# Modulation vectors by multiply-and-sum along rows on the vector engine instead of matrix products: all of layer 1's and two thirds of layer 0's, the latter in the delta-rule part

## The chip, the cores and the metric

The kernel runs on one core of a Trainium2 chip. The core has a matrix engine (PE, with its weight loads shown apart as PEld), a vector engine (DVE), a scalar engine (ACT), a general engine (POOL) and a sync engine (SP) that here does nothing but start DMA transfers. Each engine works through its own list of instructions strictly in that list's order; an instruction whose inputs are late holds up everything behind it in the same list. The metric is the device time of one execution in microseconds (us), as a median over runs.

## The reference, cut to what matters

Two layers run over 512 latent tokens and 256 context tokens of 1024 channels. In each layer every normalisation and every residual is modulated by six vectors per token kind, which come from one condition vector for the latent tokens (`c`) and one for the context tokens (`c_ctx`):

```
def adaln_modulation(cond, w_mod, b_mod):
    m = jax.nn.silu(cond) @ w_mod + b_mod          # (1024) @ (1024, 6144) + (6144)
    return jnp.split(m[..., None, :], N_MOD, axis=-1)
...
    sh1, sc1, g1, sh2, sc2, g2 = adaln_modulation(c, w_mod[layer], b_mod[layer])
    csh1, csc1, cg1, csh2, csc2, cg2 = adaln_modulation(c_ctx, w_mod[layer], b_mod[layer])
    h = rmsnorm(x, norm1_g[layer]) * (1.0 + sc1) + sh1
    ...                                             # input projection, three mixers, merge
    x = x + g1 * mix
    x = x + g2 * sq_relu_mlp(rmsnorm(x, norm2_g[layer]) * (1.0 + sc2) + sh2, ...)
```

`sh1` and `sc1` are needed at the start of a layer, `g1`, `sh2`, `sc2`, `g2` only after the mixers. The last layer's context tokens need `csh1` and `csc1` alone. The three mixers of a layer are a state-space scan (S5), a windowed attention, and a gated delta rule, which inverts small triangular matrices and then takes 12 sequential steps over chunks of tokens.

## The kernel before

All weights come from DRAM in tiles of 128 x 1024 floats (512 KB). `load_w` (L221) brings one in by SP's queue (tile `ws`, three buffers, L217), rounds it on ACT (`wh`, L227) and forms the rest on DVE (`wl`, L228; in some parts on POOL); a product is then three PE passes into PSUM (`pg`, L178: `wh` with the high part of the activations, `wl` with the high part, `wh` with the low part). The tiles `wh` and `wl` have two buffers each.

The modulation vectors of a layer are 6144 numbers for two token kinds. `adaln` (L241) makes them in 12 blocks of 512 columns. A block is four transfers of 512 KB (`wa`, SP's queue), eight PE products that stream 512 columns each with the 32 columns of conditions (`conds`) as weights, in 32-column strips of PE (L251, 16 rows of the profile to a block since each 32-bit product counts twice), one ACT scaling (`ms`, L254), four PE transposes (L257), and two short DVE instructions (`md`, `modv`). `adaln` is a generator: each `drain` puts one more block into the program. Layer 0's blocks 2, 3, 0, 1 stand at the start. Layer 0's blocks 4 to 11 stand in the conv part of layer 0, one before the keys of the attention and one behind each projection with its convolution (`conv`). Layer 1's 12 blocks stand in layer 0's MLP, one at every second of the up products; the tables for layer 1's scan (`s5_tables`, many short DVE instructions) stand there too.

Layer 0 goes in this order, by the profile's time: start and input projection for the scan (to about 214 us); the conv part, in which DVE carries the S5 scan (L669 to L672, a chain of short instructions) and PE the projections (to about 395); the attention (to about 597); the delta-rule part (`dn_main`, to about 920); the merge of the three mixers (to about 1110); and the MLP (to about 1760), which has four groups of eight up products and eight down products. Layer 1 follows.

The delta-rule part has these steps. *Prep*: the keys are transposed, their square sums taken on DVE (`dsq`, L1022), masks multiplied (`dD`, `dLT`, `dQK`). SP then writes the triangular blocks to DRAM and reads them back in another layout (`dl`, `dN`). *Inversion*: 31 rounds of a product and a subtraction on DVE for both directions (`dtm` L1123, `dPi` L1125). SP writes the inverse out and reads it back (`dp`, `dq`, `dLT`, `dPT`), PE and DVE join the blocks (L1147, L1157, `dLT` L1164). *Core*: 12 sequential steps of small PE products with DVE, ACT and POOL between. *Out*: normalisation and transposes. Since this chain leaves PE free for long stretches, 28 large products that nothing there waits for (the gates, `gates` in `mixers`) are put between by `place`: its plan `G0` gives for each a mark (an instruction of the chain), behind which the scheduler may put it. Eight of them have the mark `p5`, the last product of the prep, so that they cover the inversion.

A scheduler decides the order on each engine from the order in the program, these marks and its own model of durations.

Of the kernel before, what the change touches and what calls it, by code (L numbers as in the profile page):

```python
# [8 lines left out]
F32 = mybir.dt.float32  # L9
F32R = mybir.dt.float32r  # L10
I32 = mybir.dt.int32
AF = mybir.ActivationFunctionType
OP = mybir.AluOpType
# [4 lines left out]
NL = 2  # L18
# [15 lines left out]
SM_G1, SM_G2, SM_GF, SM_BM, SM_CV, SM_DG, SM_SK, SM_AL, SM_DT, SM_D = 0, 16, 32, 40, 136, 256, 258, 274, 290, 306  # L34
# [6 lines left out]
def pack(inp):  # L41
    import numpy as np

    f = {k: np.asarray(v) for k, v in inp.items()}
    o = {}

    def feat(a):
# [6 lines left out]
    cond[:, 1] = f["c_ctx"]  # L54
    o["cond"] = feat(cond.T)
    o["wmod"] = np.ascontiguousarray(
        f["w_mod"].reshape(NL, 4, 2, 128, 12, 512).transpose(0, 4, 1, 3, 2, 5).reshape(NL, 12, 4, 128, 1024))

    cg = (128 * np.arange(4)[:, None, None] + 16 * np.arange(8) + np.arange(16)[:, None]).reshape(-1)
    idx = list(cg)  # L60
# [64 lines left out]
    t = np.arange(128)[:, None]  # L125
# [56 lines left out]
def setup(g):  # L182
    tc, nc, A = g.tc, g.nc, g.A
    es = g.es
    g.base = es.enter_context(tc.tile_pool(name="base", bufs=1))
    g.wp = es.enter_context(tc.tile_pool(name="wp", bufs=2))
    g.ps = es.enter_context(tc.tile_pool(name="ps", bufs=1, space=PSUM))
    g.dr = es.enter_context(tc.tile_pool(name="dr", bufs=1, space=DRAM))
    g.ca = g.base.tile([128, CA_N], F32, name="ca")
    nc.sync.dma_start(g.ca, A["ca"])  # L190
    g.sm = g.base.tile([128, SM_N], F32, name="sm")
    nc.sync.dma_start(g.sm, A["small"])
    g.ident = g.ca[:, CA_ID:CA_ID + 128]
    g.ones = g.base.tile([128, 32], F32, name="ones")
    nc.gpsimd.memset(g.ones, 1.0)
    g.cneg = g.base.tile([128, 1], F32, name="cneg")
    nc.gpsimd.memset(g.cneg, -0.5)
    g.cpos = g.base.tile([128, 1], F32, name="cpos")
    nc.gpsimd.memset(g.cpos, 0.5)
    g.hpi = g.base.tile([128, 1], F32, name="hpi")  # L200
    nc.gpsimd.memset(g.hpi, math.pi / 2)
    g.modv = g.base.tile([128, NL, 48, 2], F32, name="modv")
    g.g1 = g.base.tile([128, 8, 2], F32, name="g1a")
    g.g2 = g.base.tile([128, 8, 2], F32, name="g2a")

# [26 lines left out]
def cond_setup(g):  # L232
    nc = g.nc
    c = g.p5a[1].tile([128, 8, NCH], F32, name="cond", tag="uy", bufs=2)[:, :, :32]
    nc.sync.dma_start(c, g.A["cond"])
    g.cs = g.base.tile([128, 8, 32], F32, name="conds")
    nc.scalar.activation(g.cs, c, AF.Tanh, scale=0.5)
    nc.vector.scalar_tensor_tensor(g.cs, g.cs, 1.0, c, op0=OP.add, op1=OP.mult)


def adaln(g, l, nbs, pool, bufs=2):  # L241
    nc = g.nc
    for nb in nbs:
        ps = pm(g, "s")
        for kp in range(4):
            w = pool.tile([128, 1024], F32, name="wa", tag="wa", bufs=bufs)
            g.ad_last = nc.sync.dma_start(w, g.A["wmod"][l, nb, kp])
            for k2 in range(2):
                kt = kp * 2 + k2
                c = kt % 4  # L250
                nc.tensor.matmul(ps[32 * c:32 * c + 32, :], lhsT=g.cs[:, kt, :], rhs=w[:, k2 * 512:k2 * 512 + 512],  # L251
                                 start=kt < 4, stop=kt >= 4, tile_position=(0, 32 * c))
        ms = pool.tile([128, 512], F32, name="ms", tag="ms", bufs=1)
        nc.scalar.mul(ms, ps, 0.5)  # L254
        p2 = pm(g, "s")
        for j in range(4):
            nc.tensor.transpose(p2[:, j * 128:j * 128 + 128], ms[:, j * 128:j * 128 + 128], g.ident)  # L257
        md = pool.tile([128, 4, 2], F32, name="md", tag="md", bufs=1)
        nc.vector.tensor_reduce(md, raw(p2, 0, [[128, 4], [1, 2], [32, 4]]), axis=AX.X, op=OP.add)
        bm = g.sm[:, SM_BM + 48 * l + nb * 4:SM_BM + 48 * l + nb * 4 + 4]  # L260
        nc.vector.tensor_tensor(g.modv[:, l, nb * 4:nb * 4 + 4, :], md,
                                bm[:, :, None].to_broadcast([128, 4, 2]), op=OP.add)
        yield


def drain(it, n=1):
    for _ in range(n):
        next(it, None)
# [1032 lines left out]
def mixers(g, l, hp):  # L1301
    g.marks = {}
    nc, tc, A = g.nc, g.tc, g.A
    cx = l < NL - 1
# [77 lines left out]
    if cx:  # L1382
# [6 lines left out]
        pa = pa_.__enter__()  # L1389
        with tc.tile_pool(name=f"a1{l}", bufs=1, side="right", reuse_waits="tile") as a1:  # L1390
            att_setup(g, l, pa, pa, a1, cx)
            ad = adaln(g, 0, range(4, 12), a1, AD1)
            drain(ad)
            att_kv()
            for x, i in enumerate(list(range(4, 12)) + list(range(4))):
                conv(i, a1, CDV0[x])
                drain(ad)
                if x in HS:
                    with tc.issue_after(g.wl_last) if HI else nullcontext():
                        g.hst.pop(0)()  # L1400
            bat = dn_ba(g, l, a1)
# [9 lines left out]
        pa_.__exit__(None, None, None)  # L1411
        s5_close()
        g.wle = nc.vector

        def fill(wh):
            if wh == "out":
                place(g, gt, G0, H0, sum(GU0.values()))

        dn(bat, fill)
        fl_.__exit__(None, None, None)  # L1420
        hp[0].__exit__(None, None, None)
    else:
# [276 lines left out]
def mlp(g, l, out):  # L1699
# [4 lines left out]
    if cx:  # L1704
        tb = s5_tables(g, l + 1, lambda k, d: nc.vector, 1)
    with tc.tile_pool(name=f"ml{l}", bufs=1, reuse_waits="tile") as pool:
        ad = adaln(g, l + 1, range(12), pool)
        def up(js, grps):
            ws = [load_w(g, l, W_F1 + j) for j in js]
            rs = [pool.tile([128, nn], F32, name="rl", tag="rl", bufs=2) for _ in js]  # L1710
# [11 lines left out]
        for gi in range(4):  # L1722
            hid = []
            for j in range(8):
                if gi > 0 or j > 1:
                    up([8 * gi + j], groups(cx))
                elif j == 0:
                    up([0, 1], [[p] for p in passes(cx)])
                if cx:
                    drain(ad, j % 2)  # L1730
                    drain(tb)
            last = gi == 3 and not cx
            if last:
                g.mp_.__exit__(None, None, None)
                last_group(g, l, pool, hid, out)
                break
            sts = [Stats(g, pool, p.n, 2, ("rl", nn), "ms", p.key) for p in P_LC] if cx and gi == 3 else None
            ws = {}
            order = [(m, p) for m in range(8) for p in (P_LC if cx else P_LC[:1])]
            if sts:  # L1740
                order = order[:12] + [(m, p) for p in P_LC for m in (6, 7)]
            for m, p in order:
                if m not in ws:
                    ws[m] = load_w(g, l, W_F2 + 8 * gi + m)
                ff2(g, l, ws[m], m, p, hid)
                if sts:
                    sts[P_LC.index(p)].add(m, g.x[:, m, p.sl])
                    if m == 7:
                        st = sts[P_LC.index(p)]
                        g.pbs.append(st.bcast())  # L1750
                        if PF and p.key == "l":
                            st.pace(PF)
                        else:
                            g.plan = []
# [90 lines left out]
```

## Time and profile before

| | |
|---|---|
| median of three runs | 2936.27 us (2933.69, 2936.27, 2941.55) |
| the profiled execution | 2948.86 us, of which the span of the instructions is 2947.1 us |
| PE busy | 2703.7 us, 92% of the span |
| PEld busy | 2190.6 us, 74% |
| DVE busy | 1664.9 us, 56% |
| ACT busy | 908.2 us, 31% |
| POOL busy | 595.6 us, 20% |
| DMA transfers | 343.61 MB, mean 117 GB/s |

Busy time is the union of an engine's instructions; products on PE overlap, so that 100% busy is not PE at its peak. Durations in the text are from the one profiled execution, which was 12.6 us longer than the median.

### The profile page before, as it was taken

What the parts mean: (1) busy time and instruction counts of PE and PEld (TensorE: products, weight loads), DVE (VectorE), ACT (ScalarE), POOL (GpSimd) and SP (SyncE); (2) the same over time, 40 slices, a digit from 0 to 9 for tenths busy, and PEclk for the clock granted to TensorE, in tenths of its full rate; (3) what the DMA queues carried; (4) which work ended last, traced back from release to release, by engine and by line L of the source; (5) the groups of instructions that cost most, each with busy time, mean ns of one, the idle gap of its engine ahead of it and who ended that gap; (6) DMA issues with size and microseconds to landing.
All of it is one profiled execution on the core that took longest, in us unless ns stands there. A gap on an engine that the chain in (4) does not pass through costs nothing.

```text
span 2947.1 us, 46158 instructions
## 1 busy us (share of the span) xinstructions
PE 2703.7 (92%) x17844; PEld 2190.6 (74%) x17844; DVE 1664.9 (56%) x4335; ACT 908.2 (31%) x1643; POOL 595.6 (20%) x765
## 2 busy tenths in 40 slices
PE   4698799999999999999999999758996999999998
PEld 1585578878677788787778878646775768889997
DVE  7839984345336647747432334996457368444443
ACT  2243343233222323223121324332342233323322
POOL 4643331030213300000000011532253133100001
PEclk8799898799999999999999999878997999999999
DMA  6564422236116433535341234123433226232222
GB/s 225 154 229 159 141 72 87 69 117 172 54 39 200 132 120 115 164 120 152 118 135 66 67 113 157 65 71 116 139 100 79 95 69 213 88 99 95 94 94 72
DMA packets 206619, 343.61 MB, mean 117 GB/s; under 512 B 89280, under 2 KB 121152, under 8 KB 206400
## 3 DMA queue, kind: packets, MB, share of 16 engines
q1 hardware_dynamic: 171712, 297.56, 31.5%
q0 software_dynamic: 9600, 36.71, 3.8%
q10 hardware_dynamic: 25088, 6.40, 1.0%
q8 instruction: 140, 2.29, 0.3%
q14 instruction: 79, 0.65, 0.1%
HBM read 269.04 MB, written 68.16 MB: 114 GB/s over the span
## 4 chain that ended last, share of the span: by engine, by line
PE 66%; DVE 10%; issue 3%; POOL 1%; DMA 1%; ACT 1%; SPq 1%; POOLq 0%; DVEq 0%; ACTq 0%
PE pg L178 46%; PE pg L1577 4%; DVE rt L669 2%; PE ps L697 1%; DVE st L672 1%; PE ps L251 1%; PE pm L1200 1%; DVE rt L671 1%; PE pm L1231 1%; PE ps L849 1%; PE pm L1209 1%; PE ps L858 1%; PE pg L1627 1%; PE ps L1246 1%; PE ps L1219 1%
## 5 line engine op out<-in xcount | busy, mean ns | idle before, releaser
L228 DVE TENSOR_TENSOR wl<-ws,wh 128x1024 fp32r<-128x1024 f32 x234 | 291.9, 1249 | 339.0 <-ACT wh L227 303.7
L227 ACT CAST wh<-ws 128x1024 fp32r<-128x1024 f32 x272 | 284.9, 1049 | 609.6 <-PE pg L178 473.9
L178 PE MATMUL pg<-hhil,wh 128*128 128x512 f32 x720 | 296.2, 412 | 52.4 <-ACT cxp L884 35.2
L178 PE MATMUL pg<-hlol,wh 128*128 128x512 f32 x720 | 293.7, 408 | 0.7 <-DVE hlol L367 0.7
L178 PE MATMUL pg<-hhil,wl 128*128 128x512 f32 x720 | 292.3, 406 | 0.0
L178 PE MATMUL pg<-hlo,wh 128*128 128x512 f32 (+1 forms) x800 | 282.5, 353 | 6.2 <-DVE hlo L367 6.2
L178 PE MATMUL pg<-hh,wh 128*128 128x512 f32 (+1 forms) x832 | 284.9, 344 | 3.0 <-DVE x L1674 2.6
L178 PE MATMUL pg<-hhi,wh 128*128 128x512 f32 (+1 forms) x800 | 283.0, 354 | 4.9 <-ACT cxp L884 4.9
L178 PE MATMUL pg<-hh,wl 128*128 128x512 f32 (+1 forms) x832 | 284.2, 343 | 1.0 <-DVE wl L228 1.0
L178 PE MATMUL pg<-hl,wh 128*128 128x512 f32 (+1 forms) x832 | 283.7, 342 | 0.0
L178 PE MATMUL pg<-hhi,wl 128*128 128x512 f32 (+1 forms) x800 | 280.5, 351 | 0.0
L178 PEld LDWEIGHTS pg<-hhil,wh 128*128 128x128 f32 x720 | 139.4, 194 | 97.1 <-ACT cxp L884 36.7
L1674 DVE SCALAR_TENSOR_TENSOR x<-pg,modv,x 128x512 f32<-128x512 f32 (+1 forms) x104 | 64.9, 626 | 246.0 <-PE pg L178 245.7
L178 PEld LDWEIGHTS pg<-hlo,wh 128*128 128x128 f32 x800 | 155.9, 195 | 37.4 <-issue 13.8
L178 PEld LDWEIGHTS pg<-hh,wh 128*128 128x128 f32 x832 | 157.3, 189 | 30.1 <-issue 8.3
L178 PEld LDWEIGHTS pg<-hhi,wh 128*128 128x128 f32 x800 | 155.7, 195 | 31.6 <-issue 8.8
L178 PEld LDWEIGHTS pg<-hhi,wl 128*128 128x128 f32 x800 | 155.6, 195 | 29.4 <-issue 11.5
L178 PEld LDWEIGHTS pg<-hh,wl 128*128 128x128 f32 x832 | 157.4, 189 | 24.5 <-issue 4.1
L178 PEld LDWEIGHTS pg<-hl,wh 128*128 128x128 f32 x832 | 157.4, 189 | 23.3 <-issue 5.6
L178 PEld LDWEIGHTS pg<-hhil,wl 128*128 128x128 f32 x720 | 139.2, 193 | 35.9 <-issue 4.8
L178 PEld LDWEIGHTS pg<-hlol,wh 128*128 128x128 f32 x720 | 139.2, 193 | 35.3 <-issue 4.9
L178 PE MATMUL pg<-hhic,wh 128*128 128x256 f32 x400 | 114.2, 286 | 3.9 <-ACT cxp L884 3.0
(438 smaller groups left out, 6019.9 us busy)
## 6 DMA issues: line engine op xcount, KB each, us to landing
ws<-in_wt SPq DMA_DIRECT2D x272, 512.0 KB, 3.6
wa<-in_wmod SPq DMA_DIRECT2D x96, 512.0 KB, 4.4
gtd<-gr POOLq DMA_DIRECT2D x24, 384.0 KB, 2.9
tg<-gtd POOLq DMA_DIRECT2D x24, 384.0 KB, 3.4
tb<-tC SPq DMA_DIRECT2D x64, 128.0 KB, 2.3
cvd<-ctp SPq DMA_DIRECT2D x20, 384.0 KB, 2.6
gtd<-gr POOLq DMA_DIRECT2D x24, 256.0 KB, 2.5
tg<-gtd POOLq DMA_DIRECT2D x24, 256.0 KB, 3.0
```

The source lines that it names most:

```text
L178: g.nc.tensor.matmul(ps, lhsT=wt[:, a], rhs=x(k), start=i == 0, stop=i == n - 1)
L227: nc.scalar.copy(hi, s)
L228: g.wle.tensor_tensor(lo, s, hi.bitcast(F32), op=OP.subtract)
L251: nc.tensor.matmul(ps[32 * c:32 * c + 32, :], lhsT=g.cs[:, kt, :], rhs=w[:, k2 * 512:k2 * 512 + 512], start=kt < 4, stop=kt >= 4, tile_pos ...
L669: v.tensor_tensor(t1, view(k - 1), A12[:, 0], op=OP.mult)
L671: v.tensor_tensor(t1, t1, view(k), op=OP.add)
L672: v.tensor_tensor(view(k), t1, t2, op=OP.add)
L697: nc.tensor.matmul(o, lhsT=gm[pp, k * 128:k * 128 + 128], rhs=st[pp, k // 2, k % 2, pr, c0:], start=False, stop=k == 3)
L849: nc.tensor.transpose(p[:, x * 128:x * 128 + 128], Ps[kv][:, i * 128:i * 128 + 128], g.ident)
L858: mi = nc.tensor.matmul(po[64 * kv:64 * kv + 64, :128], lhsT=a.v[:, kt, 64 * kv:64 * kv + 64], rhs=PT[:, 2 * i + kv, :], start=i == 0, sto ...
L1577: nc.tensor.matmul(ps, lhsT=wt[:, a], rhs=x[:, k, sl], start=i == 0, stop=i == 11)
L1674: g.nc.vector.scalar_tensor_tensor(g.x[:, m, sl], acc, g.modv[:, l, 40 + m, p.r:p.r + 1], g.x[:, m, sl], op0=OP.mult, op1=OP.add)
```

## The change

Twenty of the 24 blocks are no longer made by PE. A second copy of the modulation matrix is kept transposed in DRAM (`wmodt`): a tile there is 128 output features on the partitions by the 1024 inputs along the row. The two condition vectors lie beside it, repeated on all partitions (`condr`, 1 MB). A new generator, `adaln_rows`, makes their silu once (two ACT and two DVE instructions of 128 x 1024) and then, for each tile, one transfer of 512 KB and one DVE instruction `tensor_tensor_reduce` of 128 x 1024 for each token kind, which multiplies the tile by the condition and sums along the row, onto the bias, straight into `modv`. In the profile such an instruction is followed by a short one that reads the accumulator out.

Layer 0's blocks 4 to 11 become 32 tiles with two instructions each (64 in all). They leave the conv part and go into the delta-rule part, two tiles with each of the first eight gates and one with each later one, in a pool with one buffer for `wa` and one for the product `wo`. Since they are drained inside `place`, they stand behind the same marks as the gates. Layer 1's blocks become 48 tiles, of which 16 have two instructions and 32 have one (64 in all), two buffers for `wa`, in layer 0's MLP: two tiles with each of the first 20 up products, one with the others. The four blocks at the start stay.

```
+def adaln_rows(g, l, tiles, nr, pool, bufs=2):
+    nc = g.nc
+    c = pool.tile([128, 2, 1024], F32, name="condr", tag="condr", bufs=1)
+    nc.sync.dma_start(c, g.A["condr"])
+    for r in range(2):
+        w = pool.tile([128, 1024], F32, name="wa", tag="wa", bufs=bufs)
+        nc.scalar.activation(w, c[:, r], AF.Tanh, scale=0.5)
+        nc.vector.scalar_tensor_tensor(c[:, r], w, 1.0, c[:, r], op0=OP.add, op1=OP.mult)
+    yield
+    for t in tiles:
+        w = pool.tile([128, 1024], F32, name="wa", tag="wa", bufs=bufs)
+        nc.sync.dma_start(w, g.A["wmodt"][48 * l + t - 16])
+        b = SM_BM + 48 * l + t
+        for r in range(nr(t) - 1, -1, -1):
+            o = pool.tile([128, 1024], F32, name="wo", tag="wo", bufs=1) if r else w
+            nc.vector.tensor_tensor_reduce(o, w, c[:, r], 0.5, g.sm[:, b:b + 1], op0=OP.mult, op1=OP.add,
+                                           accum_out=g.modv[:, l, t, r:r + 1])
+        yield
...
             att_setup(g, l, pa, pa, a1, cx)
-            ad = adaln(g, 0, range(4, 12), a1, AD1)
-            drain(ad)
             att_kv()
             for x, i in enumerate(list(range(4, 12)) + list(range(4))):
                 conv(i, a1, CDV0[x])
-                drain(ad)
...
         g.wle = nc.vector
+        ad_ = tc.tile_pool(name=f"ad{l}", bufs=1, side="right", reuse_waits="tile")
+        ad = adaln_rows(g, l, range(16, 48), lambda t: 2, ad_.__enter__(), 1)
+
+        def gates_ad():
+            for i, _ in enumerate(gt):
+                drain(ad, 2 if i < 8 else 1)
+                yield
 
         def fill(wh):
             if wh == "out":
-                place(g, gt, G0, H0, sum(GU0.values()))
+                place(g, gates_ad(), G0, H0, sum(GU0.values()))
+                drain(ad, 40)
...
-        ad = adaln(g, l + 1, range(12), pool)
+        if cx:
+            ad = adaln_rows(g, l + 1, range(48), lambda t: 2 if t < 16 else 1, pool)
...
-                    drain(ad, j % 2)
+                    drain(ad, 1 + (j + 8 * gi < 20))
```

What the scheduler makes of it is shown at three places. The first is DVE's list in the inversion of layer 0 (`dtm` and `dPi` are the rounds of the inversion in its two directions, `wl` belongs to a gate's weights). Before, some rounds in a row stand so:

```order
L1123 TENSOR_TENSOR dtm_5836<-dN_5780,dPi_5781 96x192
L1123 TENSOR_TENSOR dtm_5839<-dN_5789,dPi_5790 96x192
L1125 TENSOR_TENSOR dPi_5781<-dPi_5781,dtm_5836 96x24x8
L1125 TENSOR_TENSOR dPi_5790<-dPi_5790,dtm_5839 96x24x8
L1123 TENSOR_TENSOR dtm_5842<-dN_5780,dPi_5781 96x207
L1123 TENSOR_TENSOR dtm_5845<-dN_5789,dPi_5790 96x207
L228 TENSOR_TENSOR wl<-ws,wh 128x1024
L1125 TENSOR_TENSOR dPi_5781<-dPi_5781,dtm_5842 96x23x9
L1125 TENSOR_TENSOR dPi_5790<-dPi_5790,dtm_5845 96x23x9
```

Now:

```order
L1146 TENSOR_TENSOR dtm_5606<-dN_5568,dPi_5569 96x135
L284 ISA wo,modv<-wa,condr,sm 128x1024
L284 ISA modv 128x1
L1148 TENSOR_TENSOR dPi_5578<-dPi_5578,dtm_5597 96x29x3
L1148 TENSOR_TENSOR dPi_5569<-dPi_5569,dtm_5606 96x27x5
L284 ISA wa,modv<-wa,condr,sm 128x1024
L284 ISA modv 128x1
L1146 TENSOR_TENSOR dtm_5603<-dN_5577,dPi_5578 96x112
L1146 TENSOR_TENSOR dtm_5612<-dN_5568,dPi_5569 96x156
L1148 TENSOR_TENSOR dPi_5578<-dPi_5578,dtm_5603 96x28x4
L1148 TENSOR_TENSOR dPi_5569<-dPi_5569,dtm_5612 96x26x6
L231 TENSOR_TENSOR wl<-ws,wh 128x1024
```

Between the first and the last round of the inversion stand 18 of the new instructions (nine pairs) and seven `wl`; before there were four `wl`. Of the other 46, three stand ahead of the first square sum (`dsq`), 11 between it and the last `dQK`, six between that and the first round, seven between the last round and the last joining copy `dLT`, and 19 in the first steps of the core (counted in the whole list, by the new instruction's line).

The second place is SP's list of transfers, from the write of the triangular blocks (`dl`) to the write of the inverse (`dp`). Before:

```order
L1107 DMA dl<-dLT 32x24x32 x8
L1357 DMA dvf<-cvd_1081 128x768 x2
L217 DMA ws<-in_wt 128x1024
L1111 DMA dN_5780<-dl 96x1024
L1111 DMA dN_5789<-dl 96x1024
L1380 DMA dzg<-zgd_1082 128x768 x2
L217 DMA ws<-in_wt 128x1024 x5
L1128 DMA dp<-dPi_5781 96x1024
```

Now:

```order
L1130 DMA dl<-dLT 32x24x32 x8
L280 DMA wa<-in_wmodt 128x1024
L1380 DMA dvf<-cvd_1082 128x768 x2
L220 DMA ws<-in_wt 128x1024
L280 DMA wa<-in_wmodt 128x1024
L1134 DMA dN_5568<-dl 96x1024
L1134 DMA dN_5577<-dl 96x1024
L280 DMA wa<-in_wmodt 128x1024
L220 DMA ws<-in_wt 128x1024
L280 DMA wa<-in_wmodt 128x1024
L220 DMA ws<-in_wt 128x1024
L280 DMA wa<-in_wmodt 128x1024
```

The list goes on in that way, one `wa` to one `ws`, up to the write of the inverse, and behind the 14 transfers of the inverse ten more `wa` stand ahead of the next `ws`. With one buffer, each `wa` waits until both instructions on the tile before it are done.

The third place is DVE's list at the end of the scan in the conv part (`rt` and `st` are the scan, `aP` and `aM` the attention's scores and maxima, `gr` a gate). Before:

```order
L669 TENSOR_TENSOR rt_2144<-st,A_1337 128x64
L670 TENSOR_TENSOR rt_2145<-st,A_1337 128x64
L671 TENSOR_TENSOR rt_2144<-rt_2144,st 128x64
L751 TENSOR_TENSOR arf<-arf,ash 128x512
L672 TENSOR_TENSOR st<-rt_2144,rt_2145 128x2x32
L825 ISA aP,aM<-pm,cb,sm 128x384
```

Now:

```order
L1390 SCALAR_TENSOR_TENSOR gr<-gr,pg 128x256
L695 TENSOR_TENSOR st<-rt_2139,rt_2140 128x2x32
L862 TENSOR_SCALAR aP<-aP,aM 128x256 x2
L1391 TENSOR_SCALAR gr<-gr 128x768
L692 TENSOR_TENSOR rt_2145<-st,A_1338 128x64
L693 TENSOR_TENSOR rt_2146<-st,A_1338 128x64
L694 TENSOR_TENSOR rt_2145<-rt_2145,st 128x64
L695 TENSOR_TENSOR st<-rt_2145,rt_2146 128x2x32
L851 ISA aP,aM<-pm,cb,sm 128x256
```

Ahead of the scan's last instruction stood two maxima of the first kind (L825) and two of the second (L828); now there are eight and ten, and the first gates' instructions. Work of the attention has moved ahead of the end of the scan.

## Rows read from the trace of the kernel before

**Rows 1.** The page: busy time, and chain that ended last by line

```profile
PE 2703.7 (92%) x17844; PEld 2190.6 (74%) x17844; DVE 1664.9 (56%) x4335; ACT 908.2 (31%) x1643; POOL 595.6 (20%) x765
...
PE pg L178 46%; PE pg L1577 4%; DVE rt L669 2%; PE ps L697 1%; DVE st L672 1%; PE ps L251 1%; PE pm L1200 1%; DVE rt L671 1%; PE pm L1231 1%; PE ps L849 1%; PE pm L1209 1%; PE ps L858 1%; PE pg L1627 1%; PE ps L1246 1%; PE ps L1219 1%
```

**Rows 2.** Chain that ended last, in 1110 to 1760 us, by line

```profile
by line: PE pg L178 86.6%; PE ps L251 6.0%; PE ps L585 2.5%; PE pm L286 1.1%; PE ps L575 1.1%; PE ps L257 0.8%; issue 0.5%; PE pm L319 0.3%; PE pm L327 0.2%; DVE x L1674 0.2%; DVE nt L357 0.2%; ACT wh L227 0.1%; ACT ssumc L293 0.1%; ACT ms 
```

**Rows 3.** L251, then L257: stretch, PE and PEld busy, clock, DMA

```profile
1110.00:1760.00 650.00, 42.58 (x192) 6.25 (x192) 1.00 0.36 113
1110.00:1760.00 650.00, 7.18 (x48) 5.87 (x48) 1.00 0.36 113
```

**Rows 4.** Stretches of the span; the first row names the columns

```profile
core 0: us, PE busy (x) PEld busy (x) DVE busy (x) ACT busy (x) POOL busy (x), PEclk, DMA share, GB/s
1116.00:1347.00 231.00, 231.00 (x1343) 181.82 (x1342) 158.35 (x671) 65.82 (x114) 3.41 (x5) 1.00 0.45 135
1347.00:1760.00 413.00, 409.85 (x2309) 334.20 (x2307) 158.84 (x388) 98.41 (x147) 14.14 (x12) 1.00 0.32 101
220.00:395.00 175.00, 143.43 (x724) 100.32 (x723) 169.85 (x468) 59.73 (x86) 64.95 (x59) 0.87 0.39 139
395.00:595.00 200.00, 193.83 (x1326) 165.33 (x1326) 96.08 (x299) 73.74 (x177) 31.22 (x75) 0.86 0.23 75
```

**Rows 5.** Longest wait of PE in 1110 to 1760 us: us, times, longest

```profile
PE pg L178 <- DVE x L1674: 0.9, 2, 0.6
```

**Rows 6.** Stretches of the delta-rule part (columns as rows 4)

```profile
632.00:664.00 32.00, 28.87 (x223) 23.54 (x222) 26.82 (x98) 8.92 (x18) 16.94 (x21) 1.00 0.23 75
664.00:684.00 20.00, 20.00 (x124) 17.67 (x123) 2.66 (x3) 10.06 (x30) 3.17 (x6) 1.00 0.75 194
684.00:723.00 39.00, 39.00 (x229) 34.10 (x228) 38.25 (x129) 9.24 (x14) 2.16 (x4) 1.00 0.42 143
723.00:738.00 15.00, 15.00 (x90) 12.54 (x88) 2.45 (x2) 2.94 (x6) 1.08 (x2) 1.00 1.05 219
738.00:754.00 16.00, 10.85 (x408) 9.39 (x409) 5.65 (x9) 3.03 (x6) 3.40 (x9) 0.77 0.22 84
754.00:893.00 139.00, 138.87 (x1191) 98.93 (x1190) 51.46 (x157) 33.55 (x85) 25.42 (x54) 0.99 0.13 42
```

**Rows 7.** DVE in the delta-rule part, in order: start, duration, what

```profile
633.01 0.28 DVE L1022 CUSTOM_DVE_ANT_0 dsq<-ktok 128x128 f32<-128x128 f32 x1
633.22 0.08 DVE L1022 DVE_READ_ACCUMULATOR2_ANT dsk<- 128x1 f32 x1
633.34 0.29 DVE L1022 CUSTOM_DVE_ANT_0 dsq<-ktok 128x128 f32<-128x128 f32 x1
...
684.01 0.20 DVE L1123 TENSOR_TENSOR dtm<-dN,dPi 96x31 f32<-96x31 f32 x1 [1.20 <-DMA dN<-dl]
...
720.29 0.30 DVE L1125 TENSOR_TENSOR dPi<-dPi,dtm 96x31 f32<-96x31 f32 x2
...
747.04 4.56 DVE L1164 COPY dLT<-pm 32x512 f32<-32x512 f32 x8 [14.23 <-PE pm L1157]
```

**Rows 8.** SP's issues for the inverse: start, length of the batch, what

```profile
720.54 0.80 SPq L1128 DMA_DIRECT2D dp<-dPi  x2
...
734.17 1.13 SPq L1138 DMA_DIRECT2D dPT<-dq  x1
```

**Rows 9.** The page: a group of DVE, and a group of transfers

```profile
L228 DVE TENSOR_TENSOR wl<-ws,wh 128x1024 fp32r<-128x1024 f32 x234 | 291.9, 1249 | 339.0 <-ACT wh L227 303.7
...
wa<-in_wmod SPq DMA_DIRECT2D x96, 512.0 KB, 4.4
```

**Rows 10.** Waits of DVE in 590 to 920 us: us, times, longest

```profile
DVE dS L1239 <- PE pm L1231: 49.8, 18, 5.7
```

**Rows 11.** The scan on DVE as it begins: start, duration, what

```profile
214.03 1.86 DVE L669 TENSOR_TENSOR rt<-st,A 128x64 f32<-128x64 f32 x1
215.82 0.26 DVE L670 TENSOR_TENSOR rt<-st,A 128x64 f32<-128x64 f32 x1
```

More of the change, by code (lines that the diff above doesn't have):

```diff
@@ L56, in pack @@
     o["wmod"] = np.ascontiguousarray(
-        f["w_mod"].reshape(NL, 4, 2, 128, 12, 512).transpose(0, 4, 1, 3, 2, 5).reshape(NL, 12, 4, 128, 1024))
+        f["w_mod"].reshape(NL, 4, 2, 128, 12, 512).transpose(0, 4, 1, 3, 2, 5)[0].reshape(12, 4, 128, 1024)[:4])
+    o["wmodt"] = np.ascontiguousarray(f["w_mod"].transpose(0, 2, 1).reshape(NL * 48, 128, 1024)[16:])
+    o["condr"] = np.ascontiguousarray(np.broadcast_to(np.stack([f["c"][0], f["c_ctx"]]), (128, 2, 1024)))
     cg = (128 * np.arange(4)[:, None, None] + 16 * np.arange(8) + np.arange(16)[:, None]).reshape(-1)
@@ L202, in setup @@
     g.modv = g.base.tile([128, NL, 48, 2], F32, name="modv")
+    nc.gpsimd.memset(g.modv[:, 1, :, 1], 0.0)
     g.g1 = g.base.tile([128, 8, 2], F32, name="g1a")
@@ L235, in cond_setup @@
     nc.sync.dma_start(c, g.A["cond"])
-    g.cs = g.base.tile([128, 8, 32], F32, name="conds")
+    g.cs = g.p5a[1].tile([128, 8, 32], F32, name="conds")
     nc.scalar.activation(g.cs, c, AF.Tanh, scale=0.5)
@@ L246, in adaln @@
             w = pool.tile([128, 1024], F32, name="wa", tag="wa", bufs=bufs)
-            g.ad_last = nc.sync.dma_start(w, g.A["wmod"][l, nb, kp])
+            g.ad_last = nc.sync.dma_start(w, g.A["wmod"][nb, kp])
             for k2 in range(2):
@@ L1413, in mixers @@
         g.wle = nc.vector
+        ad_ = tc.tile_pool(name=f"ad{l}", bufs=1, side="right", reuse_waits="tile")
[4 more added lines that the diff above has]
+                yield
         def fill(wh):
             if wh == "out":
-                place(g, gt, G0, H0, sum(GU0.values()))
+                place(g, gates_ad(), G0, H0, sum(GU0.values()))
+                drain(ad, 40)
         dn(bat, fill)
+        ad_.__exit__(None, None, None)
         fl_.__exit__(None, None, None)
```

## The prediction

> **What bounds the kernel now.** I read the busy times first: PE is busy for 92% of the span and DVE for 56% [rows 1], so work moved from PE to DVE looks free. The list of the chain that ended last says the same of the whole, PE's big products (L178) at 46% [rows 1]. But the share is an average over stages, and the change touches four, so I read each by itself.
>
> In the MLP of layer 0 PE is the limit: the products L178 are 86.6% of the chain there, L251 6.0% and L257 0.8% [rows 2]; PE is busy 231.00 of the first 231 us and DVE 158.35, falling to 158.84 of the next 413 [rows 4]. PE's longest wait there is 0.9 us in two times [rows 5].
>
> In the conv part it is the other way round: DVE is busy 169.85 of 175 us, PE 143.43 at a clock of 0.87; in the attention behind it PE is busy 193.83 of 200 and DVE 96.08 [rows 4].
>
> The delta-rule part is a chain that changes engines. In the prep (632 to 664 us) DVE is busy 26.82 of 32; in the inversion (684 to 723) DVE is busy 38.25 of 39 and nothing else is in the chain; PE is busy for all of it, 39.00, but with gates, and in the 15 us behind it again 15.00 [rows 6]. That cover has no slack: the last round ends at 720.6 [rows 7], SP's issues of the inverse end at 735.3 [rows 8], and from 738 to 754 PE is busy only 10.85 of 16 at a clock of 0.77 [rows 6], while DVE waits 14.23 us for PE's joining product [rows 7]. In the core (754 to 893) PE is full at 138.87 of 139, DVE has 51.46 [rows 6] and its longest waits are for PE, 49.8 us in 18 [rows 10].
>
> **The price of one new instruction.** The trace has no multiply-and-sum of 128 x 1024. The nearest in size is `wl`, two inputs from SBUF and 128 x 1024 out: 1.25 us on the mean [rows 9]. The nearest in form is `dsq`, 128 x 128: 0.28 us and a read of the accumulator of 0.08, the next starting 0.33 behind [rows 7]. Below it can't be less than `wl`'s 1.23 us; above, eight times 0.33 is 2.6, which counts the fixed part eight times. I take `wl`'s 1.25, less the overlap of instruction and successor and plus the read, 1.3 us, since width decides more than form. 64 of them are 83 us in either place. A transfer `wa` takes 4.4 us to land [rows 9].
>
> **MLP, layer 1's blocks.** Removed are L251 and L257: 42.58 and 7.18 us of PE's busy time [rows 3], or 6.8% of 650 us on the chain [rows 2], 44 us. I take 46 between the two. The Trainium skill ("Perfetto Trace Analysis", section "Identifying the Most-Contended Engine") says that the busy time of matrix products is a poor measure, because they are pipelined, and asks for the share of weight loads instead; by those, 6.25 and 5.87 us in the same rows, the stage would save 12 us and the sum below would be 34 us higher. The chain, which counts only what the next product waited for, bears out the 44.
> Added are 83 us of DVE and two preparing instructions. By the order they lie in the first three of the MLP's eight stretches (about 19, 28 and 19 of them), where DVE has 158.35 us of 231 already [rows 4]; the scheduler moves part of the table work later, and by counts of rows I get 63, 79 and 74 us in three stretches of about 77. That is nearly full, and `wl` of the next weight stands in the same list with only two buffers. PE will wait now and then, which it does not today: 5 to 20 us, I take 9. Net -37 (-49 to -25).
>
> **Conv part and attention, layer 0's blocks out.** About two thirds of 50 us of PE work go, but DVE sets the pace here and loses only two short instructions to a block. So the gain is indirect: attention work moves ahead of the end of the scan. Six more pairs of maxima there are some 3.5 of the attention's 24 pieces, 200 us / 24 = 8.3 each: 29 us; two gates of about a piece each make it 46. DVE has 49 more instructions ahead of the scan's last one, at 0.36 us on the mean (169.85 / 468 [rows 4]) up to 0.57 for the attention's larger ones: 18 to 28 us by which the scan ends later. Net -18; the bounds are -5 (if the scan is held up more) and -30 (about all the PE work that is gone).
>
> **Delta-rule part, layer 0's tiles in.** Prep: 11 new instructions between the first square sum and the last `dQK`, 14.3 us; DVE's idle time there is 5.2 us [rows 6], of which half may hide some; each second one waits for a load that starts only when its buffer is free, +3 us. +15 (11 to 18). From there to the first round: six more, 7.8 us, most beside the write and read of the blocks, but `wl` of the covering gates stands behind them, and so PE's products ahead of the read: +7 (3 to 9). Inversion: 18 x 1.3 = 23.4, three more `wl` at 1.15 = 3.5, and waits for `wa`, which takes 4.4 us to land while the list holds some 4 us of rounds between two pairs, +4: +31 (26 to 39). Nothing hides it: PE's cover holds the same gates as before and ends about when it ended. Behind the inversion: `dLT` now stands behind six of the new instructions, whose three tiles load one after the other behind SP's 14 issues; of the 14.23 us that DVE waits there today most is used: +6 (3 to 9). Core: 19 x 1.3 = 25 us in the first steps, half of it in waits of DVE for PE, half in the chain's way: +12 (8 to 25); here PE also restarts from a longer stop, at a low clock as from 738 on. Sum +71 (45 to 97).
>
> **Sum.** 71 - 37 - 18 = +16 us. The profiled execution took 2948.9 us, so 2965 in its terms; it lay 12.6 us above the median, so 2952 as a median.
>
> **Rivals.**
> *The other side: the delta part pays only the bare instructions.* Then 29 x 1.3 in prep and inversion, less the 5.2 us of idle time, plus 3.5 for `wl`: +36, with MLP -46 and conv -18: -28, 2908. For it: PE is busy with gates throughout, and in the core DVE has room. Against it: the gates are fixed in number, and the loads have one buffer. It decides if the delta part grows by under 46 us (37 and 18, less the 9 us that can be told).
> *Even:* the delta part grows by about 55, 2936.
> *DVE fills up in the MLP.* If the tables stayed where they were, 158 + 83 = 241 us of DVE would stand against about 200 of PE, and the saving falls to some 10: +43, 2979. The order moves the tables, which speaks against it.
> *Loads set the pace.* One tile is 4.4 of load, 2.6 of work and some 0.7 to issue, 7.7 us; 32 tiles are 246 us against the 261 from 632 to 893. With a `ws` queued behind each waiting `wa`, gates come late as well: the delta part +95, 2976.
> *DVE and POOL hold each other up.* As the scan begins, one instruction takes 1.86 us and the next of the same shape 0.26 [rows 11]. If the new ones meet POOL as often as POOL is busy, 53% of the prep and 18% of the core [rows 6], at 1.6 us each: 11 x 0.53 x 1.6 + 19 x 0.18 x 1.6 = 15 us more, 2967. The Trainium skill ("SBUF — State Buffer", section "Who interferes with whom") says that a DVE instruction with two inputs from SBUF and a GpSimd instruction that reads SBUF share a port, and whoever is first holds it for the whole instruction.
>
> **Chances.** The forecast 0.38, the other side 0.25, even 0.15, DVE full in the MLP 0.10, loads 0.07, port 0.05. A measurement of this kernel tells about 0.3%, 9 us, from no change. Faster: the 0.25 and 0.04 of the forecast's lower tail, 0.29. Same: 0.15 and another 0.04, 0.19. Slower: 0.52. The likeliest case by itself has the terms' half ranges of 26, 12 and 12, as independent 31: 2921 to 2983. The range reaches to the other side's 2908 nearly and over the cases at 2976 and 2979: 2910 to 2988.
>
> **What would show it.** Right: the stretch from the first square sum to the first joining copy about 59 us longer, with DVE full in the inversion for 67 us in place of 36.6, PE idle 40 us or more ahead of the joining products, the MLP some 37 us shorter with waits of PE for `wl`, the attention's end about 18 us earlier. Wrong: a new instruction far from 1.3 us; PE finding other work in the inversion; the MLP shorter by over 45 or under 20.

## The result, and the profile after

| | runs | median | lowest to highest |
|---|---|---|---|
| before | 20 | 2943.93 us | 2923.46 to 2959.61 |
| after | 20 | 2966.10 us | 2943.55 to 2978.38 |

The ratio is 1.0077, with a 95% interval from 1.0055 to 1.0099: 22 us slower. Single executions of either kernel differ by over 1%, and the two that were profiled lie badly for a direct comparison: that of before (2948.86 us) is above its median, that of after (2943.55 us) is the fastest of its 20. Their difference, -5.3 us, has the wrong sign, so the two traces are compared stage by stage, and each stage's length is checked against the other kernels' traces below.

The page of the changed kernel, with its busy times and its chain, answers to [rows 1]:

```profile
PE 2611.0 (89%) x17444; PEld 2154.5 (73%) x17444; DVE 1820.9 (62%) x4555; ACT 898.3 (31%) x1627; POOL 602.1 (20%) x766
...
PE pg L180 41%; PE pg L1606 4%; DMA wa<-in_wmodt 3%; DVE st L695 1%; DVE rt L692 1%; DVE wa L284 1%; DVE wo L284 1%; PE ps L720 1%; DVE wl L231 1%; PE pm L1223 1%; DVE rt L694 1%; PE ps L872 1%; PE pm L1254 1%; PE ps L881 1%; PE pm L1232 1%
```

PE lost 93 us of busy time and DVE gained 156. New in the chain are the transfers `wa` at 3%, about 88 us, and the new instructions themselves (L284) at 1% for either form. The new instruction's own lines (count, duration in ns, lowest, median and highest):

```profile
L284 DVE CUSTOM_DVE_ANT_0 wa<-wa,condr,sm x80: 1265/1280/1444, 587.6 to 1389.0; 128x1024 f32<-128x1024 f32 x80
L284 DVE CUSTOM_DVE_ANT_0 wo<-wa,condr,sm x48: 1265/1285/1637, 586.2 to 1275.8; 128x1024 f32<-128x1024 f32 x48
```

Stretches of the changed kernel, with the columns of [rows 4], answer to those and to [rows 6]: prep, way to the inversion, inversion, way to the joining copies, core; then the MLP's first three stretches and its rest.

```profile
598.00:642.00 44.00, 32.59 (x234) 26.47 (x233) 40.73 (x122) 8.55 (x18) 22.06 (x22) 0.88 0.37 128
642.00:662.00 20.00, 20.00 (x127) 17.79 (x126) 8.44 (x14) 10.48 (x31) 3.23 (x6) 1.00 0.88 237
662.00:736.00 74.00, 54.56 (x306) 46.67 (x304) 63.63 (x169) 12.90 (x20) 3.78 (x7) 0.89 0.49 164
736.00:769.00 33.00, 8.53 (x396) 7.50 (x397) 15.25 (x25) 0.98 (x2) 2.81 (x8) 0.50 0.57 140
769.00:925.00 156.00, 150.97 (x1256) 109.92 (x1253) 77.43 (x210) 35.70 (x89) 28.96 (x56) 0.97 0.22 74
1150.00:1382.00 232.00, 224.13 (x1269) 186.74 (x1268) 210.44 (x615) 64.96 (x108) 3.42 (x5) 0.98 0.58 182
1382.00:1760.00 378.00, 375.93 (x2140) 317.71 (x2138) 180.26 (x549) 92.76 (x141) 13.52 (x11) 1.00 0.27 84
```

The inversion takes 74 us where it took 38, and in it DVE is no longer busy throughout: 63.63 of 74. The rest it mostly waits for the new tiles; from 662 to 736 us its waits are (us, times, longest):

```profile
DVE wo L284 <- DMA wa<-in_wmodt: 10.2, 8, 2.8
```

Three things thus make up the 36 us: 18 new instructions, whose successors start 1.21 us behind them (22 us), three more `wl` of 1.25 us (4 us), and these waits (10 us). PE runs out of gates (54.56 of 74) and stands almost still behind it (8.53 of 33, at a granted clock of 0.50, the lower of its two levels, 1.2 GHz). PE's longest waits, from 598 to 925 us and from 915 to 1145:

```profile
PE pm L1170 <- DMA dPT<-dq: 31.0, 3, 26.2
...
PE pg L1606 <- ACT yh L1312: 19.4, 1, 19.4
```

The first is the joining product, which waits for the inverse; before, PE was idle for only 5 of the 16 us around it [rows 6]. The second was not in the prediction at all: at the start of the merge PE waits for its first input, `yh`, which ACT makes from the loaded tile `tg`. In the MLP PE is idle for some 8 us of 232, where it was idle for none.

The lengths of the stages come from the first and last starts of one line in each trace, taken apart: prep from the first `dsq` to the last `dQK`; way from there to the first round; inversion; joining from the last round to the last `dLT` copy; core from there to the first normalising sum (`dms`); out and merge from there to the first residual (`x` L1660); MLP from there to the last `x` of the down products (L1674). "Att." is the time at which the attention's last product starts. The kernels e1 to e10 are the experiments below.

| | att. | prep | way | inversion | joining | core | out, merge | MLP |
|---|---|---|---|---|---|---|---|---|
| before | 602.6 | 30.3 | 19.3 | 37.8 | 30.8 | 145.4 | 165.3 | 694.1 |
| after | 569.6 | 42.6 | 21.7 | 73.5 | 31.9 | 156.8 | 171.9 | 661.9 |
| e1 | 599.9 | 30.3 | 19.5 | 37.6 | 31.8 | 145.5 | 163.0 | 660.1 |
| e2 | 583.3 | 30.4 | 19.4 | 37.7 | 31.1 | 146.3 | 164.0 | 662.6 |
| e3 | 574.0 | 42.8 | 21.6 | 73.0 | 31.3 | 156.7 | 172.4 | 694.0 |
| e4 | 591.7 | 30.1 | 17.7 | 37.8 | 31.4 | 174.6 | 182.9 | 660.5 |
| e5 | 599.6 | 30.4 | 19.7 | 37.4 | 31.1 | 146.1 | 172.6 | 694.1 |
| e6 | 594.5 | 44.0 | 21.4 | 76.3 | 32.6 | 155.3 | 162.6 | 658.7 |
| e7 | 583.6 | 41.6 | 22.9 | 71.3 | 35.1 | 145.9 | 173.0 | 662.6 |
| e8 | 597.7 | 30.3 | 19.3 | 37.8 | 31.9 | 145.4 | 165.3 | 660.6 |
| e9 | 596.7 | 64.8 | 19.0 | 37.5 | 30.5 | 147.0 | 175.2 | 661.8 |
| e10 | 585.8 | 66.2 | 16.4 | 62.4 | 27.9 | 146.6 | 173.5 | 661.9 |

All stages but the attention repeat to some 4 us between kernels that share them. The end of the attention doesn't: 583 to 603 us in five kernels with layer 0's blocks in the conv part, 570 to 597 in seven without.

### The profile page after: what moved, and what is told of

Same layout as the page of the kernel before. It is cut to its first block, busy times and chain, and to the rows that moved or that the text cites. A ratio compares the mean times of both kernels' runs of the same rounds, so it can differ in the third digit from the quotient of the medians.

```text
span 2941.8 us, 45530 instructions
## 1 busy us (share of the span) xinstructions
PE 2611.0 (89%) x17444; PEld 2154.5 (73%) x17444; DVE 1820.9 (62%) x4555; ACT 898.3 (31%) x1627; POOL 602.1 (20%) x766
## 3 DMA queue, kind: packets, MB, share of 16 engines
q1 hardware_dynamic: 172000, 299.66, 31.8%
## 4 chain that ended last, share of the span: by engine, by line
PE 58%; DVE 15%; DMA 5%; issue 3%; POOL 1%; ACT 1%; SPq 1%; ACTq 0%; POOLq 0%; DVEq 0%
PE pg L180 41%; PE pg L1606 4%; DMA wa<-in_wmodt 3%; DVE st L695 1%; DVE rt L692 1%; DVE wa L284 1%; DVE wo L284 1%; PE ps L720 1%; DVE wl L231 1%; PE pm L1223 1%; DVE rt L694 1%; PE ps L872 1%; PE pm L1254 1%; PE ps L881 1%; PE pm L1232 1%
## 5 line engine op out<-in xcount | busy, mean ns | idle before, releaser
L180 PEld LDWEIGHTS pg<-hhil,wh 128*128 128x128 f32 x720 | 139.8, 194 | 92.6 <-ACT cxp L907 37.8
L1703 DVE SCALAR_TENSOR_TENSOR x<-pg,modv,x 128x512 f32<-128x512 f32 (+1 forms) x104 | 64.8, 626 | 197.9 <-PE pg L180 197.6
L180 PEld LDWEIGHTS pg<-hhil,wl 128*128 128x128 f32 x720 | 139.5, 194 | 37.8 <-issue 3.8
L1606 PE MATMUL pg<-yh,wh 128*128 128x512 f32 (+1 forms) x288 | 104.8, 366 | 25.9 <-ACT yh L1312 21.7
```

The source lines that it names most:

```text
L180: g.nc.tensor.matmul(ps, lhsT=wt[:, a], rhs=x(k), start=i == 0, stop=i == n - 1)
L1606: nc.tensor.matmul(ps, lhsT=wt[:, a], rhs=x[:, k, sl], start=i == 0, stop=i == 11)
L1703: g.nc.vector.scalar_tensor_tensor(g.x[:, m, sl], acc, g.modv[:, l, 40 + m, p.r:p.r + 1], g.x[:, m, sl], op0=OP.mult, op1=OP.add)
```

## The experiments

Each ratio is to the kernel before, timed again beside the experiment.

**The two halves apart (e1, e2, e3).** e1 keeps layer 1's half alone; layer 0's blocks go back to PE in the conv part:

```diff
+            ad = adaln(g, 0, range(4, 12), a1, AD1)
+            drain(ad)
...
+                drain(ad)
...
-        ad_ = tc.tile_pool(name=f"ad{l}", bufs=1, side="right", reuse_waits="tile")
-        ad = adaln_rows(g, l, range(16, 48), lambda t: 2, ad_.__enter__(), 1)
...
-                place(g, gates_ad(), G0, H0, sum(GU0.values()))
-                drain(ad, 40)
+                place(g, gt, G0, H0, sum(GU0.values()))
```

> Layer 1's modulation by rows on DVE in the MLP, layer 0's blocks on PE in the conv part as before, conditions in their old place in memory. Theory (the stages add up: MLP -32 us, nothing else moves): ratio to the kernel before 0.989, 0.985 to 0.992; MLP from the first to the last square of the up products some 32 us shorter than the 534.5 us of before. Rival (the MLP's saving is eaten by waits of PE for wl, and the shorter MLP of the changed kernel's profile was one lucky execution): 0.996 or more.

Measured: 0.9902 (0.9870 to 0.9934), and an MLP of 660.1 us, 34 less than before. The theory held.

e2 is e1 but with the conditions (`conds`) in the other pool, as the change has them:

```diff
-    g.cs = g.base.tile([128, 8, 32], F32, name="conds")
+    g.cs = g.p5a[1].tile([128, 8, 32], F32, name="conds")
```

> As the first, but with the tile of conditions moved to another pool as in the change; nothing of layer 0 moved. In this order SP's loads tg stand behind the writes ybd at the end of the delta-rule part, as in the changed kernel and not as in the one before. Theory (the 17 us lost at the start of the merge come from these late loads, by where tiles lie in memory, not from the new instructions): about 17 us above the first, ratio 0.994, with a wait of PE of 15 us or more for yh. Rival (the merge was late because of the new instructions in the delta-rule part): as the first, 0.989, and no such wait.

Measured: 0.9894 (0.9860 to 0.9928). The order that the expectation names was not the one this kernel had: in its trace `tg` is issued at 872.85 us, ahead of `ybd` at 902.06. So it shows only that the place of `conds` costs nothing that can be told here, and decides nothing on the merge; e5 and e6 do.

e3 keeps layer 0's half alone; layer 1's blocks go back to PE in the MLP, with their conditions made there anew:

```diff
-            ad = adaln_rows(g, l + 1, range(48), lambda t: 2 if t < 16 else 1, pool)
+            ad = adaln(g, l + 1, range(12), pool)
...
-                    drain(ad, 1 + (j + 8 * gi < 20))
+                    drain(ad, j % 2)
```

> Layer 0's eight blocks by rows in the delta-rule part as in the change, layer 1's 12 blocks on PE as before (their conditions made anew in the MLP). Theory: conv part and attention -33 us or somewhat less, delta-rule part +53, merge +17: +37 to +54 us, ratio 1.013 to 1.018, and above the changed kernel's 1.008. Rival (the layer 0 move pays for itself and the loss is elsewhere): 1.000 to 1.005.

Measured: 1.0157 (1.0125 to 1.0190). Its stages are those of the changed kernel up to the merge, and its MLP is that of before to 0.1 us. The two halves add up: -0.98% and +1.57% make +0.59%, against +0.77%, with intervals of some 0.3 each way for the halves and 0.22 for the whole. Layer 1's half wins 1%, layer 0's move loses 1.6%.

**The new instructions out of DVE's chain (e4).** All of layer 0's sums stand behind the last joining copy on DVE:

```diff
+            g.marks["dvi"] = v.tensor_copy(LT[pp, d, b0:b1, oc:oc + 32], pz[...]...).ins
...
-                place(g, gates_ad(), G0, H0, sum(GU0.values()))
-                drain(ad, 40)
+                place(g, gt, G0, H0, sum(GU0.values()))
+                with tc.issue_after(g.marks["dvi"]):
+                    drain(ad, 40)
```

> The changed kernel, but all of layer 0's multiply-and-sums queued on DVE behind the last joining copy dLT, so that prep and inversion are as before. Theory (DVE's own chain in prep and inversion carries the loss): of the +53 us in the delta-rule part about 12 in the prep and 36 in the inversion go away, the core and what follows get 15 to 25 more: 25 to 30 us below the changed kernel, ratio to before 0.998. Rival (loads with one buffer and SP's queue carry the loss, wherever the instructions stand): no better than the changed kernel, 1.008.

Measured: 0.9974 (0.9956 to 0.9993), 1.0% below the changed kernel. Prep, way and inversion are those of before; the core is 29 us longer than before, 18 longer than in the changed kernel, and out and merge are 11 longer than in the changed kernel. In the core and out (737 to 950 us) DVE's and PE's longest waits are

```profile
DVE wo L284 <- DMA wa<-in_wmodt: 60.2, 29, 4.1
...
PE pm L1300 <- DVE dO L1291: 24.8, 6, 8.5
```

so that here, too, DVE stands still for loads in front of its own chain. The theory held in sum, but what follows the inversion became 29 us longer, not 15 to 25: the core is no free place for the new instructions.

**The merge (e5, e6).** e5 is the kernel before with an unused tile where the change has its pool (POOL writes one column of it, twice):

```diff
+        pd_ = tc.tile_pool(name=f"pd{l}", bufs=1, side="right", reuse_waits="tile")
+        pd = pd_.__enter__().tile([128, PADN], F32, name="pad")
+        nc.gpsimd.memset(pd[:, :1], 0.0)
...
+PADN = 3840
```

> The kernel before with nothing changed but an unused tile of 15 KB on each partition, held through the delta-rule part where the change holds its own pool. SP's order then has the loads tg behind the writes ybd, as in the changed kernel. Theory (the 17 us lost at the start of the merge come from where the pool lies: the merge's first tiles have to wait for memory): merge about 17 us later, PE waiting some 15 to 20 us for yh, ratio 1.006. Rival (the new instructions delay the merge): as before, 1.000, no such wait.

Measured: 1.0048 (1.0021 to 1.0076). PE's wait at the start of the merge is there without a single new instruction, and out and merge take 172.6 us, as in the changed kernel:

```profile
PE pg L1583 <- ACT yh L1289: 16.0, 1, 16.0
```

SP's list in that trace has the loads of the merge's first input behind the writes of the delta rule's result:

```profile
922.52 3.00 SPq L1381 DMA_DIRECT2D ybd<-dyb  x2
925.57 4.15 SPq L1598 DMA_DIRECT2D tg<-ycd  x4
```

In the kernel before, the loads stood ahead:

```profile
890.98 3.03 SPq L1592 DMA_DIRECT2D tg<-ycd  x4
920.20 0.33 SPq L1381 DMA_DIRECT2D ybd<-dyb  x1
```

In the changed kernel they are issued at 957.08 us, 7 us behind the last `ybd`. e6 is the changed kernel with its pool on the other side of the memory:

```diff
-        ad_ = tc.tile_pool(name=f"ad{l}", bufs=1, side="right", reuse_waits="tile")
+        ad_ = tc.tile_pool(name=f"ad{l}", bufs=1, reuse_waits="tile")
```

> The changed kernel with the pool of the multiply-and-sum on the other side of the memory; the new instructions stay in prep, inversion and core, and SP's loads tg stand ahead of the writes ybd again. Theory: the merge's 17 us come back, 1.002 to the kernel before. Rival (they belong to the new instructions): 1.008 as the changed kernel.

Measured: 1.0039 (1.0013 to 1.0064). `tg` is issued at 943.61 us, ahead of `ybd` at 973.99, the wait is gone and out and merge take 162.6 us. The sums stand nearly where they stand in the changed kernel (18 in the inversion, as there). So the place of the pool, not the arithmetic, delays the merge. In all twelve traces the wait, 13 to 20 us, is there where the loads `tg` stand behind the writes `ybd`, and is not there where they stand ahead. Its price is smaller than the 17 us that I had read from the first trace: from the merge's first product to its first residual it then takes 134 to 136 us in place of 143 to 145 (141 in e4, which has sums there). Out and merge together are 7 to 9 us longer.

**Instruction or load (e7, e9, e10).** e7 has one sum on each tile in place of two, with the same loads; the context tokens' modulation is left out:

```diff
-        ad = adaln_rows(g, l, range(16, 48), lambda t: 2, ad_.__enter__(), 1)
+        ad = adaln_rows(g, l, range(16, 48), lambda t: 1, ad_.__enter__(), 1)
```

> The changed kernel with one multiply-and-sum in place of two on each of layer 0's 32 tiles; the modulation of the context tokens is left out (zeros), the 32 loads stay. By the order 7 in place of 11 then stand in the prep, 11 in place of 18 in the inversion, none of 19 in the core. Theory (each instruction in the chain costs its 1.28 us): prep and inversion 15 to 17 us shorter, the core 8 to 12, ratio 0.998. Rival (the loads set the pace: one buffer, 4 us to land each): prep and inversion at most 5 us shorter, ratio 1.005.

Measured: 1.0060 (1.0031 to 1.0089). The core came back to that of before, but prep and inversion together are only 3.2 us shorter than in the changed kernel: the theory failed there, and the rival's "at most 5 us" held. (In the inversion stand 13 of the sums, not 11 as I had counted.) DVE's longest wait from 590 to 780 us says why:

```profile
DVE wa L284 <- DMA wa<-in_wmodt: 58.6, 27, 8.4
```

Nearly every sum stands still for its tile, 2.2 us on the mean, with the inversion's next round behind it. I bent the theory to that: an instruction costs its 1.28 us, and on top DVE waits for a load that its list expects too early. e9 gives the same kernel three buffers, in the memory that the second condition vector and `wo` leave:

```diff
-    c = pool.tile([128, 2, 1024], F32, name="condr", tag="condr", bufs=1)
+    c = pool.tile([128, nc_, 1024], F32, name="condr", tag="condr", bufs=1)
...
-        ad = adaln_rows(g, l, range(16, 48), lambda t: 1, ad_.__enter__(), 1)
+        ad = adaln_rows(g, l, range(16, 48), lambda t: 1, ad_.__enter__(), 3, 1)
```

> The seventh experiment's kernel (one multiply-and-sum on each of layer 0's 32 tiles, context modulation left out) with three buffers for the tiles in place of one, in the memory that its second condition vector and product tile leave. By the order 27 of the 32 then stand in the prep, one between prep and inversion, none in the inversion, one before it the rest. First theory, bent by the seventh (an instruction costs its 1.28 us of DVE's chain, and on top DVE stands still for the next load, since its list puts the instruction where the load is not yet there): no waits for loads, prep 32 to 36 us longer than before, inversion and core as before, from the first square sum to the first dms 32 to 38 us longer than before in place of the seventh's 53; ratio 1.000 to 1.003. Rival (the loads' own traffic or the queue's order slows this part, with any number of buffers): as the seventh, 50 us or more, 1.006.

Measured: 0.9982 (0.9952 to 1.0012). DVE's waits for these loads, from 590 to 900 us, have all but gone:

```profile
DVE wa L284 <- DMA wa<-in_wmodt: 4.8, 5, 1.9
```

The prep is 34.5 us longer than before for its 27 sums, 1.28 each, and all that follows up to `dms` is as before, 35 us in all: the bent theory held, but for "no waits". The same sums and tiles as in e7 thus cost 18 us less in this part (e7: 53). That is the price of the single buffer together with the places that come with it: with three buffers the scheduler puts nearly all sums into the prep and none into the inversion, so e9 doesn't tell the waits from the places. e10 loads a single tile for all 64 sums:

```diff
+        if l or t == tiles[0]:
             w = pool.tile([128, 1024], F32, name="wa", tag="wa", bufs=bufs)
             nc.sync.dma_start(w, g.A["wmodt"][48 * l + t - 16])
```

> The changed kernel with one tile loaded for all of layer 0's 64 multiply-and-sums, 31 of the 32 loads left out (the sums are then of that tile alone). By the order 34 stand in the prep, 10 between prep and inversion, 16 in the inversion, with seven wl as in the changed kernel, none behind. Theory (1.28 us each on DVE's chain, no waits for loads): prep 41 to 44 us longer than before, gap 3 to 8, inversion 16 x 1.28 + 3 x 1.2 = 24 us longer, core as before: 70 to 76 us in all from the first square sum to the first dms, more than the changed kernel's 63 in spite of the loads left out; ratio 1.008 to 1.012. Rival (the loads are what costs): 45 us or less, ratio 1.003 or less.

Measured: 1.0035 (1.0010 to 1.0059). The inversion is 24.6 us longer, as the theory had it (16 x 1.28 + 3 x 1.2 = 24); the prep 36 for 34 sums; but the way and the joining are 3 us shorter each, so the sum is 56 us, between the theory's 70 and the rival's 45; the ratio is the rival's. In the prep (the first row) DVE is full, and PE, which waits for it, is busy for half of the time; the second row is the inversion:

```profile
614.00:680.00 66.00, 33.27 (x238) 26.94 (x239) 65.85 (x165) 8.67 (x19) 22.13 (x22) 0.74 0.10 35
697.00:759.00 62.00, 55.60 (x323) 48.34 (x321) 58.63 (x160) 13.51 (x21) 3.78 (x7) 0.97 0.34 118
```

So theory and rival each hold a share: 60 sums without loads cost 56 us of chain, and the changed kernel's 61 sums with their loads 63.

**The MLP's remainder (e8).** e1 with the sums queued behind the squares of all 32 up products:

```diff
-                nc.vector.tensor_tensor(r, r, r, op=OP.mult)
+                g.rlm = nc.vector.tensor_tensor(r, r, r, op=OP.mult).ins
...
-                    drain(ad, 1 + (j + 8 * gi < 20))
+                    with tc.issue_after(g.rlm):
+                        drain(ad, 1 + j % 2 + (j + gi == 0))
```

> The first experiment's kernel (layer 1 by rows, layer 0 as before) with the multiply-and-sums queued behind the squares of all 32 up products rather than in the first three stretches, so that DVE is nowhere full in the MLP. Theory (of the 44 us that the removed products held on the chain some 8 to 10 are given back as waits of PE for a full DVE): PE's idle time in the MLP falls from about 10 us to 4 or less, MLP 5 us shorter, ratio 0.988 (0.985 to 0.991). Rival (the rest of the 44 was never on the path): as the first, 0.990, with the MLP's length unchanged to 2 us.

Measured: 0.9871 (0.9839 to 0.9904), which can't be told from e1's 0.9902. The MLP is 660.6 us, unchanged. In the first 230 us of the MLP, e1 above and e8 below:

```profile
1112.00:1342.00 230.00, 221.12 (x1269) 184.44 (x1268) 210.43 (x615) 64.82 (x109) 3.41 (x5) 0.99 0.60 184
```

```profile
1112.00:1342.00 230.00, 223.53 (x1274) 185.33 (x1274) 201.56 (x722) 66.72 (x115) 3.41 (x5) 0.98 0.47 134
```

PE gains 2.4 us there and no more, and the rival's "unchanged to 2 us" held. The test is weak, though: the tables moved forward into the room that the sums left, so that DVE is still busy for 201.56 us in place of 210.43. What keeps the MLP from giving all of the 44 stays open. e1 and e8 are 1.0 and 1.3% faster than the kernel before, and so beat the changed one too.

## Why the prediction was right, point by point

The direction and the size held: +16 us forecast, +22 measured (16 to 29 by the interval), and by the stages of the table the loss and the two gains are where the prediction put them. That the sum came so near is in part luck: four terms were off by 5 to 8 us, and the delta-rule part, 8 us too high, made up for 7 us in the merge that the sum did not have.

- *Price of one new instruction.* 1.3 us taken, 1.28 measured (median); its successor starts 1.21 us behind it, accumulator read included. Right.
- *MLP.* -37 forecast with 9 us of waits; the stage is 32 us shorter in the changed kernel, 34 in e1, and PE is idle for some 7 us more than before. Right, a little too large; but the waits are less for `wl` (2.1 us) than for the tables (3.0) and for the gain of a normalisation (`g1a`, 2.1). The chain's 44 us were the better measure of what PE could give: by the weight loads' 12 us the stage could not have become 32 us shorter. The Trainium skill ("Perfetto Trace Analysis", section "Identifying the Most-Contended Engine") names the share of weight loads, beside the rate of arithmetic, as a measure of how near PE is to its peak; that it is also what a removal saves was the prediction's reading, and the measurement decides against that.
- *Conv part and attention.* -18 forecast. The changed kernel's trace says -33, but that execution is the earliest of seven; the mean end of the attention is 585.1 us in the seven kernels with the move and 596.6 in the five without, -11.5, with a standard deviation of 10 and 8 us within the groups. The scan ends later, as forecast: its last instruction starts at 417 us on the mean of the seven and at 393 in the five, 24 us (18 to 28 forecast). From there to the attention's end it takes 168 us for 203, a gain of 35 where the prediction had 46; that term was the one too large. Mechanism right, size within its bounds, not settled to better than some 5 us.
- *Delta-rule part.* +71 forecast, +63 measured (326.5 for 263.6 us from the first square sum to the first `dms`). Term by term: prep +15, measured +12; way +7, measured +2; inversion +31, measured +36; joining +6, measured +1; core +12, measured +11. In the inversion the waits for `wa` were taken at 4 us and came to 10. (The bounds given for the five terms add up to 51 to 100 us, not to the 45 to 97 that stand with the sum; the range would have been the same.) PE's cover ran out as said: with the same gates it was busy for 54.56 us of the inversion's 74. In the joining the copies did slip behind the new instructions, but these ran while DVE would have waited for PE in any case: the joining product ended 26 us behind the last round, 27 before, and DVE's old wait of 14 us took them up.
- *What was missed.* Out and merge, +7: the pool of 16 KB moves the merge's first loads behind the delta rule's last writes. The prediction had no term for what a pool does to those that come after it. It could have been read from SP's list of the changed kernel.
- *The rivals.* "DVE and POOL hold each other up" fell: the new instructions take 1.265 to 1.637 us with a median of 1.28, also in the prep, where POOL is busy for half of the time, and e9's 27 sums there cost 1.28 each. By the Trainium skill's rule ("SBUF — State Buffer", section "Who interferes with whom") the two share a port pair, and the later one waits for the whole of the other's instruction. The new instructions of the changed kernel show at most 0.36 us above the median. "DVE fills up in the MLP" was wrong: the MLP gave 32 of 37 us. "Loads set the pace" was given 0.07, at +95 us; the part grew by 63, but the mechanism has a share: 10 us of waits in the inversion, and 18 us between e7 and e9. "The other side" would have needed the delta-rule part to grow by less than 46 us.
- *A wrong sentence ahead of the prediction.* The part on the change says that the new instructions stand behind the gates' marks. The gates' marks are instructions of PE, and DVE's instructions are not held by them: in e9 all 32 sums stand ahead of the inversion, though some are drained with gates whose marks lie in the core. DVE's stand wherever the scheduler's model found them ready, which is why e4 needed a mark on DVE.

The stages' sum from the table, with the attention from the means, is -11.5 - 2 (less time from its end to the first `dsq`) + 63 + 7 - 32 = +24, against +22. Layer 1, which the change doesn't touch, lies between 1181 and 1194 us in the twelve traces and is counted as unchanged. Its mean is 1184 us in the seven kernels with the move and 1190 in the five without; no run here says why, and with these 6 us the sum is +18.

## What to carry to other kernels

Work taken off the busiest engine is worth about what the stage's chain shows for it (here 32 to 34 of 44 us), and work put on an engine that looks idle costs what the stage around it makes of it: DVE was 56% busy over the span, yet 18 instructions of 1.28 us, with three more `wl` and the waits for their loads, lengthened one stage by 36 us, because there DVE was the chain. An instruction that waits for a load in an in-order list charges its wait to everything behind it, so a tile that arrives "in the background" needs buffers enough to be loaded before its place in the list comes up. And when a pool is added, look at which transfers move in the queue of the stage after it.

## What the runs showed of the hardware

- Executions of one kernel differ by 1.2% (2943.55 to 2978.38 us over 20). Over those 20 the mean granted clock of PE goes with the time, from 0.941 in the fastest to 0.928 in the slowest. The attention's end alone differs by 19 to 27 us between kernels that share that part.
- PE at a halt falls to a granted clock of 0.50 and returns late: in the changed kernel it did nothing from 724 to 745 us, at 0.50, then worked for 14.53 of the next 30 us, still at 0.50, and stood at 1.00 from 775 to 781. Before, with a shorter wait for the inverse, the mean around it was 0.77 [rows 6].
